# Eight instead of five feed-forward pairs per layer by halves, finer down pieces, and a reordered first projection

## The chip, the cores and the metric

The program runs on one core of one Trainium2 chip. The metric is device time in microseconds (us) for one execution. Shares are of TensorE (PE, with its weight loads PEld), VectorE (DVE), ScalarE (ACT), GpSimd (POOL) and SyncE (SP, which only issues loads).

## The reference, cut to what matters

```python
D_MODEL, SEQ, DEPTH, D_FF, FFN_CONV = 1024, 512, 2, 3072, 3
def _conv_ffn(x, norm, w_up, conv_w, conv_b, w_down):
    h = _rmsnorm(x, norm)
    u = jnp.einsum('btd,df->btf', h, w_up)                    # 1024 -> 2 x 3072
    gate = _causal_dwconv(u[..., :D_FF], conv_w, conv_b)      # three taps over the tokens
    hid = jax.nn.gelu(gate, approximate=True) * u[..., D_FF:]
    return jnp.einsum('btf,fd->btd', hid, w_down)             # 3072 -> 1024
def reference(x, ...):
    for layer in range(DEPTH):
        x = x + (_rglru_block if layer == 0 else _rwkv7_block)(x, ...)   # the mixer
        x = x + _conv_ffn(x, ffn_norm[layer], ...)
    return _rmsnorm(x, final_norm)
```

All is float32, for one batch of 512 tokens.

## The kernel before

A float32 product is made of three fast ones: a weight tile and an operand tile are each split into a high part (`wh`, `hi`, made on ACT by L121 or L742) and the rest (`wl`, `lo`, made on DVE by L125 or L743), and `mm3` (L81) multiplies high by high, high by low and low by high. Weights come in tiles of 512 KB into slots of 4 KB per partition (`b4`, `N4` = 21 slots), by loads on SP's queue in the order of a list, `plan`. A tile is loaded when a slot is free, and a slot is freed when the split's two halves, or the products of `wh` and `wl`, have been read.

The feed-forward stage of a layer goes through 12 **pairs** n of 256 gate and 256 value outputs. A `Whole` pair has four products, G0, U0, G1, U1 (each 24 matmuls of 512 columns). A `Halves` pair (n in `HALVES`) makes the same from seven products of 24 matmuls of 256 columns, numbered 1 to 7 (Strassen's scheme in a seven-product form over two halves of the tokens, of the inputs and of gate and value); for these the operands are made once per layer (`operands`), and the weight tiles of products 5, 6, 3 and 4 are sums of two pieces: for 5 and 4 the second piece is added by a DMA that accumulates (on POOL's queue, L207), for 3 by another one (L747), and for 6 DVE adds (L736). Before, pairs 3, 5, 7, 9 and 11 go by halves.

After every second pair, a **down** step multiplies 4 blocks of the hidden values (`hid`) of an earlier pair of pairs with `w_down`, for two groups g of 512 outputs each, in 96 matmuls; the last has 8 blocks. Behind the first 24 matmuls of it (`between`) stand products 3 and 4 of the pair. Its results are added to `x` (layer 0, L858) or `xtok` (layer 1, L847) on DVE. When product 4 has ended, DVE makes the gate (`gpad` L777, then the conv's `cv` L689), multiplies (`s` by `ge`, L782) and splits the hidden values (`hid`, L784).

`ahead(j)` writes the splits of the products up to the j-th into ACT's and DVE's queues. A scheduler sets the final order on each engine from this order and its own estimates; instructions that are pinned keep their order. Each engine runs its queue strictly in order.

At the start, blocks of `x` and pieces of `lru_w_in` land in turn; for each block ACT and DVE make a scaled, split operand `xs` (L324, L325) and add its squares to `sqacc` (L339, L340). The first group of four output blocks is then 96 matmuls, in four pieces c of two input blocks. Four tiny products with `inv_d` (`ssq`, L347) sum the squares, POOL takes the root, and `rbc` (L359) spreads it; with that DVE scales the results into `u` (L487).

Of the kernel before, what the change touches and what calls it, by code (L numbers as in the profile page):

```python
# [27 lines left out]
N4 = 21  # L28
WARM = 17

HALVES = (3, 5, 7, 9, 11)
# [40 lines left out]
class Kernel:  # L72
# [4 lines left out]
    def mm3(self, ps, w, x, start, stop, more=False):  # L77
# [4 lines left out]
        mm(wh, xh, start=start, stop=False)  # L82
        mm(wh, xl, start=False, stop=False)
        mm(wl, xh, start=False, stop=stop)
# [34 lines left out]
    def split(self, src, hi, lo, dve=False, pin=False):  # L119
# [5 lines left out]
        self.pin(self.nc.vector.tensor_tensor(lo, src, hi.bitcast(F32), ALU.subtract))  # L125
# [5 lines left out]
    def plan_weights(self):  # L131
        I = self.I
        plan = []
        self.quads = []
# [14 lines left out]
        def ffn(l):  # L149
            up, dn = ("ffn_w_up", (l,)), ("ffn_w_down", (l,))  # L150

            def gu(six):


                for n in range(2 * six, 2 * six + 2):
                    self.quads.append(len(plan))
                    a = lambda i, j: piece(up, j * 512, (1 - i) * DFF + n * 256, 4)
                    if n in HALVES:
                        for first, more in (((0, 0), None), ((1, 1), (1, 0)), ((0, 1), None), ((1, 0), (0, 0)), ((1, 1), None)):
                            plan.append((a(*first), 4, True, more and a(*more)))  # L160
                    else:
                        for i, j in ((1, 0), (0, 0), (1, 1), (0, 1)):
                            plan.append((a(i, j), 4, False, None))
                self.quads.append(len(plan))

            def dd(row, n):
                for g in range(2):
# [43 lines left out]
    def weights_split(self, upto, pin=False, between=None):  # L211
        while self.n_split < min(upto, len(self.plan)):
# [9 lines left out]
            for j in range(k) if i == 0 else [slice(0, k)]:  # L222
                self.split(raw[:, j], hi[:, j], lo[:, j], pin=pin)
                if j == 0:
                    between()
            self.splitted[i] = (hi, lo)
            self.n_split += 1
# [10 lines left out]
    def project_gen(self, xs, evac, nob=4, kb=8, kc=2, join=2, early=None, x0=0, ahead=2):  # L238
# [4 lines left out]
        for cs in [[c] for c in range(n - join)] + [list(range(max(n - join, 0), n))]:  # L243
            first = early and cs[0] == 0
            ws = [self.next_weights(1 if first else ahead) for _ in cs]
            if first:

                (wh, wl), = ws
                for o in range(nob):
                    self.mm3(pss[o], (wh[:, 0, o * P : (o + 1) * P], wl[:, 0, o * P : (o + 1) * P]), xs[0], True, False)  # L250
# [91 lines left out]
    def norm_end(self, rbs):  # L342
# [6 lines left out]
        nc.vector.tensor_scalar(ms, ps[:, :4], EPS, None, ALU.add)  # L349
# [16 lines left out]
    def load_x(self):  # L366
# [3 lines left out]
        nc.scalar.dma_start(self.x[:, 0], xT[:, 0])  # L370
        self.weights_load(1)
        nc.sync.dma_start(self.x[:, 1], xT[:, 1])
# [17 lines left out]
    def lru(self):  # L390
        nc, tc, I = self.nc, self.tc, self.I
        xs, block = self.load_x()
        with tc.tile_pool(name="lru", bufs=1) as pool:
# [5 lines left out]
            def blocks():  # L399
                for cb in range(2, KB):  # L400
                    block(cb)
                    self.squares(cb - 2)
                    yield 1
                for cb in range(KB - 2, KB):
                    self.squares(cb)
                    yield 1

# [14 lines left out]
            def gate_weights():  # L422

                lam = self.vec("lru_lambda", 0, 8)
# [3 lines left out]
                nc.vector.tensor_scalar(s, y, 2.0, None, ALU.add)  # L428
# [16 lines left out]
                bu = self.vec("lru_b_in", 8, 8)  # L445
# [5 lines left out]
                self.pin(nc.vector.tensor_scalar(nb, bu, -1.0, None, ALU.mult))  # L451
# [9 lines left out]
                self.split(graw, gh, gl)  # L461
                yield 1

            st, us, rbs = {}, {}, []

            def scale():
                root = self.norm_end(rbs)
                for step in (0, 1, 0, 0, 1):
                    if step:
                        next(root)  # L470
                    yield 1

            def first(c):
                if c == 1:
                    self.drain()
                    self.push(scale(), 1)
                    self.push(gate_weights())
                elif c == 2:
                    while not rbs:
                        self.background(1, 1)  # L480
                elif c == 3:
                    self.starting = False
# [74 lines left out]
            for g in range(2):  # L557
                self.project(xs, lambda o, ps: take(g * 4 + o, ps), after=None if g else first, rate=1.2, rate1=0 if g else 1.2, join=2 if g else 1,
                             early=None if g else lambda: block(1))
# [23 lines left out]
    def ffn(self, l, xs, finish, after=None):  # L583
        nc, tc = self.nc, self.tc
        last = l == 1
        with tc.tile_pool(name=f"ffn{l}", bufs=1) as pool:
# [72 lines left out]

            def hidden(n):  # L660
# [14 lines left out]
            class Pair:  # L675

                def __init__(pair, n):
                    pair.n, pair.gp = n, gpads[n % 2]
                    pair.w, pair.bank, pair.s = {}, {}, {}
# [45 lines left out]
            class Halves(Pair):  # L725

                order = ((1, 5, 6, 2, 7), (3, 4))

                def weights(pair, p):
                    i = quads[pair.n]  # L730
                    if p == 1:
                        self.weights_load(i + 4)
                        pair.f = dict(zip((1, 5, 2, 7), [self.loaded.pop(i + j) for j in range(4)]))
# [8 lines left out]
                    nc.scalar.copy(hi, f[p])  # L742
                    tt(lo, f[p], hi.bitcast(F32), ALU.subtract)  # L743
                    pair.w[p] = hi, lo
                    if p == 6:
# [3 lines left out]
                def product(pair, p):  # L749
# [5 lines left out]
                    for e in range(2):  # L755
                        c = slice(e * P, e * P + P)
                        for k in range(4):
                            self.mm3(ps[:, e], (hi[:, k, c], lo[:, k, c]), op[p][k], bool(name) and e + k == 0, e + k == 4, more=not name)
# [3 lines left out]
                    if p in (1, 6, 7):  # L762
                        s[p] = two(t("s", 7))
                        nc.scalar.copy(s[p], bank["A"])
                    if p == 2:
                        tt(s[1], s[1], bank["D"], ALU.add)
# [20 lines left out]
            starts = [self.quads[l * 18 + m] for m in range(18)]  # L787
# [1014 lines left out]
```

## Time and profile before

| | us |
|---|---|
| median of 3 runs (1277.37 to 1277.41) | 1277.37 |
| the profiled execution | 1278.56 |
| its span | 1276.9 |
| PE busy in the span | 1254.6 |
| DVE, ACT, POOL busy | 931.7, 639.0, 109.6 |

The profiled execution lies 1.2 us above the median, and 1.7 us above its own span. PE is at work in nearly all of the span, so a stage's length is, where PE has no gap, the sum of its matmuls. The feed-forward stage of layer 0 lies at about 195 to 540 us of the span, that of layer 1 at about 890 to 1240; between them is the RWKV mixer, ahead of them the LRU mixer.

### The profile page before, as it was taken

How to read it: one execution, taken by the hardware profiler on the slowest of the kernel's cores; microseconds unless marked ns; L12 is line 12 of the kernel's file. 1: busy time of each engine (PE TensorE's matmuls, PEld its weight loads, DVE VectorE, ACT ScalarE, POOL GpSimd, SP SyncE). 2: the span in 40 equal slices, each digit the busy share in tenths (PEclk: the TensorE clock that was granted, in tenths of full speed). 3: DMA queues.
4: the chain of work that ended last, by engine and by line, in shares of the span. 5: the costliest groups of instructions: out<-in, count | busy, mean ns of one | idle time of the engine just before them, and what ended most of it. 6: DMA issues, size and time to landing. Idle time of an engine off the chain costs nothing.

```text
span 1276.9 us, 22237 instructions
## 1 busy us (share of the span) xinstructions
PE 1254.6 (98%) x9213; PEld 1062.6 (83%) x9213; DVE 931.7 (73%) x1408; ACT 639.0 (50%) x978; POOL 109.6 (9%) x186
## 2 busy tenths in 40 slices
PE   8999999999999999999999899999999999999998
PEld 7777888989898989877778798778889888988886
DVE  6998678767676767789999967777876666666654
ACT  6697455434343434559845356545753434343442
POOL 0000000000000000010012145310000000000000
PEclk9999999999999999999999999999999999999999
DMA  6322334445454544413222112222435363535431
GB/s 223 99 83 83 99 119 113 156 108 166 99 175 89 182 83 137 149 50 109 67 75 68 35 63 88 69 72 83 134 82 185 79 188 77 190 76 190 97 126 66
DMA packets 43045, 141.42 MB, mean 111 GB/s; under 512 B 5600, under 2 KB 7904, under 8 KB 42816
## 3 DMA queue, kind: packets, MB, share of 16 engines
q1 hardware_dynamic: 37760, 122.44, 29.3%
q0 software_dynamic: 4464, 16.25, 7.4%
q8 instruction: 72, 1.18, 0.4%
q10 hardware_dynamic: 720, 1.31, 0.3%
q14 instruction: 29, 0.24, 0.1%
HBM read 135.46 MB, written 4.52 MB: 110 GB/s over the span
## 4 chain that ended last, share of the span: by engine, by line
PE 43%; DVE 6%; ACT 3%; issue 1%; POOL 0%; POOLq 0%; ACTq 0%; DVEq 0%
PE accU L81 6%; PE accG L81 6%; PE acc L81 5%; PE accA L81 4%; PE acc L842 3%; PE acc L844 3%; PE acc L843 3%; PE accF L81 2%; DVE X L1301 1%; PE accD L81 1%; PE s L1415 1%; DVE DA L1299 1%; PE acc L1247 1%; DVE wl L125 1%; PE pd L1497 1%
## 5 line engine op out<-in xcount | busy, mean ns | idle before, releaser
L125 DVE TENSOR_TENSOR wl<-raw,wh 128x1024 fp32r<-128x1024 f32 (+1 forms) x161 | 194.5, 1213 | 123.2 <-ACT wh L121 103.0
L121 ACT CAST wh<-raw 128x1024 fp32r<-128x1024 f32 (+1 forms) x161 | 166.2, 1044 | 180.0 <-PE acc L81 43.2
L81 PE MATMUL accG<-xs,wh 128*128 128x512 f32 x448 | 138.6, 391 | 0.0
L81 PE MATMUL accU<-xs,wh 128*128 128x512 f32 x448 | 138.5, 390 | 0.0
L81 PE MATMUL acc<-hid,wh 128*128 128x512 f32 x384 | 117.8, 389 | 0.0
L743 DVE TENSOR_TENSOR lo<-raw,hi 128x1024 fp32r<-128x1024 f32 x70 | 85.4, 1222 | 39.4 <-PE accU L81 32.0
L742 ACT CAST hi<-raw 128x1024 fp32r<-128x1024 f32 x70 | 73.7, 1054 | 60.5 <-PE accU L81 25.3
L81 PEld LDWEIGHTS accU<-xs,wh 128*128 128x128 f32 x448 | 83.7, 188 | 17.1
L81 PEld LDWEIGHTS accG<-xs,wh 128*128 128x128 f32 x448 | 83.6, 188 | 17.1
L81 PE MATMUL accU<-xs,wl 128*128 128x512 f32 x224 | 87.2, 389 | 0.0
L81 PE MATMUL accG<-xs,wl 128*128 128x512 f32 x224 | 87.2, 389 | 0.0
L81 PE MATMUL accA<-xt,hi 128*128 128x256 f32 x480 | 83.6, 277 | 0.0
L81 PE MATMUL acc<-xs,wh 128*128 128x512 f32 x256 | 82.5, 401 | 0.8 <-ACT xs L324 0.8
L81 PEld LDWEIGHTS acc<-hid,wh 128*128 128x128 f32 x384 | 71.3, 188 | 14.3
L689 DVE SCALAR_TENSOR_TENSOR cv<-gpad,pv,cv 128x512 f32<-128x512 f32 x96 | 69.1, 748 | 13.1 <-ACT cv L687 12.7
L842 PE MATMUL acc<-wh,hid 128*128 128x512 f32 (+1 forms) x200 | 76.8, 384 | 0.0
L844 PE MATMUL acc<-wl,hid 128*128 128x512 f32 (+1 forms) x200 | 76.8, 384 | 0.0
L843 PE MATMUL acc<-wh,hid 128*128 128x512 f32 (+1 forms) x200 | 76.8, 384 | 0.0
L81 PE MATMUL acc<-hid,wl 128*128 128x512 f32 x192 | 74.2, 389 | 0.0
L81 PEld LDWEIGHTS accA<-xt,hi 128*128 128x128 f32 x480 | 72.6, 188 | 0.0
L81 PE MATMUL accA<-xt,lo 128*128 128x256 f32 x240 | 66.4, 277 | 0.0
L81 PE MATMUL acc<-mix,wh 128*128 128x512 f32 x192 | 59.8, 393 | 1.6 <-ACT wh L121 1.6
(374 smaller groups left out, 2864.3 us busy)
## 6 DMA issues: line engine op xcount, KB each, us to landing
raw<-in_weights_dram SPq DMA_DIRECT2D x209, 512.0 KB, 3.6
raw<-in_weights_dram POOLq DMA_DIRECT2D x30, 512.0 KB, 5.3
xd<-x SPq DMA_DIRECT2D x8, 256.0 KB, 2.3
AR<-xd SPq DMA_DIRECT2D x1, 2048.0 KB, 8.6
x<-in_xT_dram SPq DMA_DIRECT2D x3, 512.0 KB, 8.0
out_dram<-xtok ACTq DMA_DIRECT2D x4, 256.0 KB, 2.1
out_dram<-xtok SPq DMA_DIRECT2D x4, 256.0 KB, 2.0
raw<-in_weights_dram SPq DMA_DIRECT2D x2, 256.0 KB, 4.2
```

The lines of the kernel that those rows point to most:

```text
L81: mm = lambda *a, **kw: self.nc.tensor.matmul(ps, *a, skip_group_check=more, **kw)
L121: put = (self.nc.vector.tensor_copy if dve else self.nc.scalar.copy)(hi, src)
L125: self.pin(self.nc.vector.tensor_tensor(lo, src, hi.bitcast(F32), ALU.subtract))
L689: nc.vector.scalar_tensor_tensor(cv, pair.gp[:, e, j : j + T], cw(j), cv, ALU.mult, ALU.add)
L742: nc.scalar.copy(hi, f[p])
L743: tt(lo, f[p], hi.bitcast(F32), ALU.subtract)
L842: nc.tensor.matmul(ps, hh[:, s], wh[:, k, m], start=kk == 0, stop=False)
L843: nc.tensor.matmul(ps, hl[:, s], wh[:, k, m], start=False, stop=False)
L844: nc.tensor.matmul(ps, hh[:, s], wl[:, k, m], start=False, stop=kk == blocks - 1)
L1247: nc.tensor.matmul(ps, hh[:, s], wh[:, k, :], start=kk + b % 2 == 0, stop=False)
L1299: nc.vector.tensor_tensor(w, A[:, s + 1 :, s : s + 1].to_broadcast([P, n, j]), X[:, s : s + 1, 0:j].to_broadcast([P, n, j]), ALU.mult)
L1301: nc.vector.tensor_tensor(X[:, s + 1 :, 0:j], X[:, s + 1 :, 0:j], w, ALU.add)
```

## The change

- `HALVES` gets 4, 6 and 8 besides: 8 of 12 pairs of each layer go by halves.
- The down step that stood after every second pair is cut in two: behind each pair from 3 to 9 (and behind pair 2) comes one group of 512 outputs, 48 matmuls: 24 between products 7 and 3, and 24 after product 4.
- Of a pair by halves, the order of products is 1, 2, 6, 5, 7 and 3, 4, where it was 1, 5, 6, 2, 7 and 3, 4. Edges of order without a semaphore (`behind`) fix some places on DVE and ACT: the sum for product 6 behind `lo2`, `lo7` behind the sum of products 1 and 2, `lo3` behind a weight split, the first down result behind the next pair's sum.
- The scratch for DMA descriptors is given as 4096 bytes, and `N4` is 24 slots.
- At the start, the first half of the first weight tile is rounded on DVE, block 1 of `x` comes by ACT's queue, the first block's products are ordered by kind, the squares of all blocks stand behind the operands of all blocks, and `ssq` moves from the middle of the third piece to behind the first output block of the fourth. Results that end before the root is there wait in a list (`taken`).

```diff
-N4 = 21
+N4 = 24
-HALVES = (3, 5, 7, 9, 11)
+HALVES = (3, 4, 5, 6, 7, 8, 9, 11)
...
-            gu(0)
-            for six in range(1, 6):
-                gu(six)
-                if six < 5:
-                    dd((six - 1) * 512, 4)
-            dd(2048, 8)
+            for n in range(12):
+                gu(n)
+                if 2 <= n < 10:
+                    dd((n // 2 - 1) * 512, 4, (n % 2,))
+            dd(2048, 8, (0, 1))
...
-        nc.scalar.dma_start(self.x[:, 0], xT[:, 0])
+        for cb in range(2):
+            nc.scalar.dma_start(self.x[:, cb], xT[:, cb])
...
                     block(cb)
-                    self.squares(cb - 2)
                     yield 1
-                for cb in range(KB - 2, KB):
+                for cb in range(KB):
                     self.squares(cb)
                     yield 1
...
+            def taken(o, ps):
+                held.append((o, ps))
+                if o == 0:
+                    self.need("squares")
+                    self.weights_split(6)
+                    next(root)
                     self.push(gate_weights())
+                elif o == 2:
+                    next(root)
+                while rbs and held:
+                    take(*held.pop(0))
...
-                order = ((1, 5, 6, 2, 7), (3, 4))
+                order = ((1, 2, 6, 5, 7), (3, 4))
...
                     if p == 6:
-                        tt(f[1], f[5], f[1], ALU.add)
+                        pair.sum = tt(f[1], f[5], f[1], ALU.add)
+                        behind(pair.sum, pair.at[2][1])
...
-            for n in range(3, 12, 2):
+            down(0, 0, 4, between)
+            ahead(at[0] + 2)
+            for n in (*range(3, 10), 11):
...
+                def between():
+                    products((n, 3))
+                    cap[0] = len(seq)
+                    if following:
+                        self.weights_load(quads[n + 1] + 4)
+                    products((n, 4))
+                    if following:
+                        ahead(at[0] + 3)
+                        held.append(pairs[n + 1].sum)
...
+                    down(n % 2, (n // 2 - 1) * 4, 4, between)
...
-    nc = _bacc.Bacc("TRN2", target_bir_lowering=False, num_devices=1)
+    nc = _bacc.Bacc("TRN2", target_bir_lowering=False, num_devices=1, dynamic_dma_scratch_size=4096)
```

Three places show what moves. The first is PE's queue in the first group of the first projection (`acc_136` to `acc_139` are its four output blocks; `xs_178`, `xs_187` are the operands of its third piece before, `xs_193`, `xs_202` those of its fourth after). Before:

```order
L81 MATMUL acc_137<-xs_187,wh_193 128x512 x2
L81 MATMUL acc_137<-xs_187,wl_194 128x512
L347 MATMUL ssq<-inv_d,sqacc 128x1 x4
L81 MATMUL acc_138<-xs_178,wh_193 128x512 x2
L81 MATMUL acc_138<-xs_178,wl_194 128x512
```

After:

```order
L81 MATMUL acc_136<-xs_202,wh_226 128x512 x2
L81 MATMUL acc_136<-xs_202,wl_227 128x512
L349 MATMUL ssq<-inv_d,sqacc 128x1 x4
L81 MATMUL acc_137<-xs_193,wh_226 128x512 x2
L81 MATMUL acc_137<-xs_193,wl_227 128x512
```

`ssq` stood behind 60 of the 96 matmuls, and now stands behind 78.

The second is DVE's queue around the first scaled results, `u`. Before:

```order
L486 COPY u<-nb 128x3 x4
L487 TENSOR_TENSOR u<-acc_136,rb 128x512
L125 TENSOR_TENSOR wl_326<-raw_239,wh_325 128x1024
L487 TENSOR_TENSOR u<-acc_137,rb 128x512
L493 TENSOR_SCALAR xr<-u,pv,cb_133 128x512
L487 TENSOR_TENSOR u<-acc_138,rb 128x512
L125 TENSOR_TENSOR wl_376<-raw_323,wh_375 128x1024
L487 TENSOR_TENSOR u<-acc_139,rb 128x512
```

After:

```order
L127 TENSOR_TENSOR wl_415<-raw_375,wh_414 128x1024
L441 TENSOR_TENSOR sp_131<-sp_131,sps 128x8
L442 TENSOR_SCALAR sp_131<-sp_131 128x8
L443 TENSOR_SCALAR sps<-pv 128x8
L444 TENSOR_TENSOR sp_131<-sp_131,sps 128x8
L127 TENSOR_TENSOR wl_467<-raw_412,wh_466 128x1024
L485 TENSOR_TENSOR u<-acc_136,rb 128x512
L485 TENSOR_TENSOR u<-acc_137,rb 128x512
L485 TENSOR_TENSOR u<-acc_138,rb 128x512
```

The four weight splits of the second group (the first two, `wl_272` and `wl_282`, stand further ahead, between the last addition of squares and `ms`, which takes the result of `ssq`) now all stand ahead of the first `u`, where they stood among and behind the `u`. Ten small instructions of 8 and 48 elements went behind the first `u`.

The third is DVE's queue behind product 4 of a pair by halves, in layer 0 (`wl` is a split for the down step, `lo` one for a product by halves, `x<-x,acc` adds a down result). Before, behind pair 3:

```order
L777 SCALAR_TENSOR_TENSOR gpad_1365<-accA,rb 128x2x256
L125 TENSOR_TENSOR wl_2278<-raw_2217,wh_2277 128x1024
L689 SCALAR_TENSOR_TENSOR cv<-gpad_1365,pv,cv 128x512 x4
L858 TENSOR_TENSOR x<-x,acc_2074 128x512
L858 TENSOR_TENSOR x<-x,acc_2075 128x512
L782 TENSOR_TENSOR s<-s,ge 128x512 x2
L858 TENSOR_TENSOR x<-x,acc_2076 128x512
L784 TENSOR_TENSOR hid<-s,hid 128x2x256 x2
L858 TENSOR_TENSOR x<-x,acc_2077 128x512
```

After, right behind the `gpad` of pair 5 (the three `lo` up to `lo_2883` are those of products 1, 2 and 6 of pair 6, `raw_2769` becomes the sum for 6, and `lo_2943` is that of product 5):

```order
L743 TENSOR_TENSOR lo_2831<-raw_2769,hi_2830 128x1024
L743 TENSOR_TENSOR lo_2835<-raw_2825,hi_2834 128x1024
L689 SCALAR_TENSOR_TENSOR cv<-gpad_1365,pv,cv 128x512 x4
L736 TENSOR_TENSOR raw_2769<-raw_2766,raw_2769 128x1024
L792 TENSOR_TENSOR s<-s,ge 128x512 x2
L743 TENSOR_TENSOR lo_2883<-raw_2769,hi_2882 128x1024
L794 TENSOR_TENSOR hid<-s,hid 128x2x256 x2
L871 TENSOR_TENSOR x<-x,acc_2771 128x512
L871 TENSOR_TENSOR x<-x,acc_2772 128x512
L871 TENSOR_TENSOR x<-x,acc_2773 128x512
L871 TENSOR_TENSOR x<-x,acc_2774 128x512
L743 TENSOR_TENSOR lo_2943<-raw_2766,hi_2942 128x1024
```

Between `gpad` and the `lo` of product 5 there are now two splits for products 1 and 2, the sum, a third split and all four additions to `x`. The same row stands behind pairs 5 to 8 of each layer, with `xtok` for `x` in layer 1; behind pairs 3 and 4 the first `lo` stands ahead of `gpad`.

## Rows read from the trace of the kernel before

**Rows 1.** The page, part 1: busy us, share of the span, instructions.

```profile
PE 1254.6 (98%) x9213; PEld 1062.6 (83%) x9213; DVE 931.7 (73%) x1408; ACT 639.0 (50%) x978; POOL 109.6 (9%) x186
```

**Rows 2.** Nine windows of 40 us in both feed-forward stages: busy us by engine, clock.

```profile
235.00:275.00 40.00, 40.00 (x209) 34.36 (x209) 24.60 (x32) 13.65 (x16) 1.73 (x2) 1.00 0.54 158
...
sum 360.00, PE 360.00 PEld 313.73 DVE 250.41 ACT 155.99 POOL 13.52; mean PE 40.00 PEld 34.86 DVE 27.82 ACT 17.33 POOL 1.50
```

**Rows 3.** Windows, PE alone: whole pair; products 1, 6, 2; 24 down matmuls; product 4.

```profile
264.05:285.81 21.76, 21.76 (x98) 1.00 0.44 95
222.72:225.59 2.87, 2.87 (x26) 1.00 0.03 7
...
228.33:231.05 2.72, 2.72 (x27) 1.00 0.61 170
231.05:233.91 2.86, 2.86 (x27) 1.00 0.62 199
...
236.65:242.10 5.45, 5.45 (x26) 1.00 0.73 256
...
244.97:247.71 2.74, 2.74 (x26) 1.00 0.46 102
```

**Rows 4.** Windows, PE alone: the seven products of pair 3, summed.

```profile
sum 19.54, PE 19.54; mean PE 2.79
```

**Rows 5.** Timeline of DVE behind product 4 of pair 3: start, us, what.

```profile
247.91 0.69 DVE L777 SCALAR_TENSOR_TENSOR gpad<-accA,rb 128x512 f32<-128x512 f32 x1 [0.31 <-PE accA L81]
248.52 1.22 DVE L125 TENSOR_TENSOR wl<-raw,wh 128x1024 fp32r<-128x1024 f32 x1
249.65 2.73 DVE L689 SCALAR_TENSOR_TENSOR cv<-gpad,pv,cv 128x512 f32<-128x512 f32 x4
252.30 1.28 DVE L858 TENSOR_TENSOR x<-x,acc 128x512 f32<-128x512 f32 x2
253.50 1.29 DVE L782 TENSOR_TENSOR s<-s,ge 128x512 f32<-128x512 f32 x2
254.70 0.69 DVE L858 TENSOR_TENSOR x<-x,acc 128x512 f32<-128x512 f32 x1
255.30 1.29 DVE L784 TENSOR_TENSOR hid<-s,hid 128x512 fp32r<-128x512 f32 x2
256.50 1.28 DVE L858 TENSOR_TENSOR x<-x,acc 128x512 f32<-128x512 f32 x2
```

**Rows 6.** Groups of DVE's instructions in layer 1's stage: busy us, mean ns.

```profile
L743 DVE TENSOR_TENSOR lo<-raw,hi 128x1024 fp32r<-128x1024 f32 x31 | 37.9, 1222 | 19.8 <-PE accU L81 16.0 <-ACT hi L742 2.9
L847 DVE SCALAR_TENSOR_TENSOR xtok<-acc,rs,xtok 128x512 f32<-128x512 f32 x32 | 23.2, 744 | 11.6 <-PE acc L844 11.6
```

**Rows 7.** DMA issues: engine, count, size, median us from issue to landing.

```profile
raw<-in_weights_dram SPq DMA_DIRECT2D x209, 512.0 KB, 3.6
raw<-in_weights_dram POOLq DMA_DIRECT2D x30, 512.0 KB, 5.3
```

**Rows 8.** Windows at the start: us, busy PE, PEld, DVE, ACT, POOL, clock, DMA.

```profile
20.60:22.68 2.08, 1.04 (x9) 0.89 (x9) 1.94 (x3) 1.85 (x6) 0.00 (x0) 1.00 0.05 22
22.68:26.18 3.50, 3.50 (x11) 2.76 (x10) 3.02 (x19) 0.00 (x0) 1.03 (x1) 0.52 0.49 157
27.94:33.38 5.44, 5.44 (x27) 4.52 (x26) 3.73 (x7) 4.49 (x5) 0.00 (x0) 1.00 0.14 39
...
40.00:80.00 40.00, 40.00 (x180) 29.15 (x180) 37.98 (x59) 34.98 (x49) 0.00 (x0) 1.00 0.30 93
```

**Rows 9.** Timeline of PE at the start: the sums of squares.

```profile
21.79 1.05 PE L347 MATMUL ssq<-inv_d,sqacc 128*128 128x1 f32 x8 [1.04 <-DVE sqacc L340]
```

**Rows 10.** Timeline of DVE at the start: before and at the first scaled result.

```profile
19.46 2.28 DVE L340 TENSOR_TENSOR sqacc<-sqacc,sq 128x512 f32<-128x512 f32 x3
...
26.26 0.17 DVE L442 TENSOR_SCALAR nsp<-sp 128x8 f32<-128x8 f32 x1
...
29.68 0.69 DVE L487 TENSOR_TENSOR u<-acc,rb 128x512 f32<-128x512 f32 x1 [1.71 <-PE acc L81]
```

More of the change, by code (lines that the diff above doesn't have):

```diff
@@ L222, in weights_split @@
             for j in range(k) if i == 0 else [slice(0, k)]:
-                self.split(raw[:, j], hi[:, j], lo[:, j], pin=pin)
+                put = self.split(raw[:, j], hi[:, j], lo[:, j], dve=i == 0 and j == 0, pin=pin)
                 if j == 0:
@@ L248, in project_gen @@
                 (wh, wl), = ws
-                for o in range(nob):
-                    self.mm3(pss[o], (wh[:, 0, o * P : (o + 1) * P], wl[:, 0, o * P : (o + 1) * P]), xs[0], True, False)
+                for part, (w, x) in enumerate(((wh, xs[0][0]), (wl, xs[0][0]), (wh, xs[0][1]))):
+                    for o in range(nob):
+                        ins = self.nc.tensor.matmul(pss[o], w[:, 0, o * P : (o + 1) * P], x, start=part == 0, stop=False)
+                        self.tc.keep_in_program_order(ins)
                 early()
@@ L461, in gate_weights @@
                 self.split(graw, gh, gl)
+                self.starting = False
                 yield 1
             st, us, rbs = {}, {}, []
[L466 to L476, printed above, removed]
-                    self.push(gate_weights())
[L478 to L482, printed above, removed]
+            root = self.norm_end(rbs)
+            held = []
+            def taken(o, ps):
[4 more added lines that the diff above has]
+                    next(root)
+                    self.push(gate_weights())
+                elif o == 2:
+                    next(root)
+                while rbs and held:
+                    take(*held.pop(0))
             def take(b, ps):
@@ L557, in lru @@
             for g in range(2):
-                self.project(xs, lambda o, ps: take(g * 4 + o, ps), after=None if g else first, rate=1.2, rate1=0 if g else 1.2, join=2 if g else 1,
-                             early=None if g else lambda: block(1))
+                self.project(xs, (lambda o, ps: take(4 + o, ps)) if g else taken, rate=1.2, join=2 if g else 1, early=None if g else lambda: block(1))
                 for b in (0, 1, 2, 3) if g == 0 else (4, 5):
@@ L658, in ffn, with behind @@
             op = {}
+            def behind(ins, prev):
+                tc.add_manual_dep(ins.ins, prev.ins.name, NOSYNC, reason="order")
             def hidden(n):
@@ L784, in product @@
                             tt(pair.hid[:, :, 1, h], x, pair.hid[:, :, 0, h].bitcast(F32), ALU.subtract)
-            starts = [self.quads[l * 18 + m] for m in range(18)]
-            quads = [starts[n // 2 * 3 + n % 2] for n in range(12)]
-            behind = [starts[n // 2 * 3 + 2] for n in range(12)]
+            quads = [self.quads[l, n] for n in range(12)]
             pairs, hids = {}, []
```

190 lines of the change are left out of this document (110 added, 80 removed).

## The prediction

> **What bounds the kernel now.** I read the page's engine shares first: PE is busy for 1254.6 us of the span, DVE for 931.7 [rows 1]. Since that is an average, the windows come next: nine of 40 us each, taken from both feed-forward stages, hold 360.00 us of PE work in 360.00 us at clock 1.00, and DVE is busy in 250.41 of them [rows 2]. So these stages, about 690 us together, are as long as their matmuls, and a matmul less is time less as long as nothing PE waits for comes late. The start is another matter: PE works 1.04 of 2.08 us and then 3.50 us at clock 0.52 [rows 8]; and from 40 to 80 us DVE is busy for 37.98 us of 40 [rows 8], so a gain of PE at the start counts there only as far as DVE's work also comes earlier.
>
> **Pairs 4, 6 and 8 by halves.** A whole pair takes PE 21.76 us [rows 3]; the seven products of a pair by halves take 19.54 [rows 4]. Each pair saves 2.22 us. Three pairs in each of two layers: 6 x 2.22 = **13.3 us**. The other order of products doesn't change their number. The down matmuls are the same ones in pieces of 24, 5.45 us each [rows 3]; the second group's pieces of 48 were already joined. Both kinds run without a gap today, so the cut is costed at nothing on PE, bounds 0 and 1 us.
>
> What hides the rest must now be checked, since the steps are closer. One step is 19.54 + 2 x 5.45 = 30.4 us of PE. DVE has in it seven `lo`, one sum and two `wl` (ten instructions of 1.22 us [rows 6], the sum taken as one of them), four `cv`, and some 14 to 16 of 512 columns at 0.60 to 0.74: about 12.2 + 2.7 + 10 = 25 us, or 82%. It fits as a sum; what matters is the order within the step.
>
> The tight place stands behind product 4 (third piece of the order). Measured from the end of product 4, which is the start of the second down piece (247.71 [rows 3]), by the pitches from one start to the next in [rows 5]: `gpad` begins at 0.20 and takes 0.61; `lo1` and `lo2` at 1.13 each (the pitch of `wl`, same shape), four `cv` 2.65, the sum 1.13, two `s` by `ge` 1.20, `lo6` 1.13, two `hid` 1.20, four additions to `x` at 0.60. `lo5` starts at 0.20 + 0.61 + 2.26 + 2.65 + 1.13 + 1.20 + 1.13 + 1.20 + 2.40 = 12.78 and ends at 14.0. PE reaches product 5 after the down piece, products 1, 2 and 6: 5.45 + 2.87 + 2.86 + 2.72 = 13.90 [rows 3], and reads `lo5` with its third matmul, 0.2 us later. So in layer 0 it is just in time, with 0 to 0.1 us lost. In layer 1 the additions are L847, 744 ns against about 690 [rows 6, 5]: 4 x 0.06 = 0.2 us later, so about 0.2 to 0.3 us is lost. That row stands behind four pairs of each layer (behind pairs 3 and 4 the first `lo` comes ahead of `gpad`, 1.13 us of slack): 4 x 0.05 + 4 x 0.25 = **1.2 us** taken. The bounds are 0 (an engine's idle in `gpad`'s place hides it) and, if every instruction were paid at its whole duration instead of at the pitch, the rival below.
>
> The next deadlines in the step by the same pitches: `lo7` ends at 12.78 + 1.13 + 0.60 + 1.22 = 15.7, and product 7 starts at 13.90 + 2.74 = 16.6: 0.9 us to spare. `lo3` ends some 1 us before the first down piece does. The loads on SP's queue: product 5's raw tile may load when product 5 of the pair before has been read, some 13.7 us before product 4 ends (2.74 + 5.45 + 2.87 + 2.74); it needs 3.6 us on SP and 5.3 on POOL [rows 7], so it is there 4.8 us before product 4 ends, and the sum asks for it 5.7 us after that: 10 us to spare. Each pair by halves has three accumulating loads on POOL's queue, 30 for ten pairs [rows 7] and 48 for sixteen; on that queue little else stands in these stages. These are costed at nothing. Other instructions queued behind a late tile would be the whole DVE row above; that is the rival on the slower side.
>
> **The 24 slots and the smaller scratch.** The slots let loads go earlier; with PE never waiting for a load in the stages [rows 2] that is worth nothing there, and in the mixers it only moves the order: 0, bounds -1.5 and +1.5. No row shows what a scratch of 4096 bytes does: bounds 0 and the slower rival's price; 0 taken, since 5.3 us per accumulating load [rows 7] leaves POOL's queue idle for about half of a step of 30.4.
>
> **The start.** PE waits 1.04 us for the last sum of squares and then runs 3.50 us at half clock [rows 8, 9], which loses 3.50 x 0.48 = 1.68. With `ssq` behind 78 matmuls instead of 60, it comes 18 x 0.227 = 4.1 us later on PE, while the squares end later too: DVE does one split (1.13) and half a tile's rounding more ahead of them, 19.46 + 2.28 + 1.5 = 23.2 [rows 10, 5], against `ssq` at about 20.7 + 4.1 = 24.8. So no wait, and no clock falls: PE gains 2.7 us. On DVE, four splits move ahead of the first `u` (4 x 1.13 = 4.5 us), ten small instructions behind it (26.26 to 29.68 - 1.71 = 27.97 holds fifteen small ones [rows 10]: about 1.1 us). The idle 1.71 us before the first `u` takes in part of it: the first `u` comes 4.5 - 1.1 - 1.7 = 1.7 us later than 29.68, and behind it stand 4.5 - 1.1 = 3.4 us less. DVE's work from there comes 1.7 us earlier. From 40 us on DVE is the fuller engine, so its figure counts: **-1.7**, bounds -4 (PE's gain, and the idle time in DVE's first 20 us used up) and 0 (the root's chain stands behind two splits; its end then sets the first `u`); below that, +1.7 if the clock falls in the new place as it did at 22.68.
>
> **The sum.** Against the profiled execution: 1278.6 - 13.3 + 1.2 - 1.7 = 1264.8; against the median, which is 1.2 us lower, 1277.4 - 13.8 = **1263.6**.
>
> **Rivals.**
> (A) DVE's row behind product 4 sets the pace. If the row costs whole durations (0.69, 1.22, 2.73, 1.29 and so on [rows 5, 6]), `lo5` ends at 0.2 + 0.69 + 4 x 1.22 + 2.73 + 2 x 1.29 + 4 x 0.69 + 1.22 = 15.1, and PE waits about 1.0 us in layer 0 and 1.2 in layer 1, in four steps each, 8.8 us. A third of it again for the steps with less slack gives 10 to 12, so about 1263.6 - 1.2 + 11 = 1273.4, from 1270 to 1276. For it: the margin is at zero, and a PE that waited lost its clock once [rows 8]. Against: in [rows 5] nine instructions of the same kinds start one behind the other at less than their durations, with no idle time between.
> [...]
> [...] By the row [rows 7], three loads of 5.3 us in a step of 30.4 don't pile up, but no row excludes a wait of POOL for scratch: (B) gets 8 in 100.
> (C) The start gives nothing, or the clock falls again: 1265.3 to 1267.
> (D) The stages lose nothing, and the start gives its full 4: 1277.4 - 13.3 - 4 = 1260.1; with the mixers' 1.5, 1258.6.
> (E) That the change doesn't do what it says: pairs stay whole. The order of PE's instructions speaks against it; 0.
>
> **How the numbers follow.** Forecast 0.55 (1261 to 1266), (C) 0.15, (D) 0.08, (A) 0.14, (B) 0.08. The range 1259.0 to 1273.0 takes in the forecast, (C), nearly all of (D) and about half of (A). About 0.2%, 2.6 us, can be told from no change: faster is below 1274.8, slower above 1279.9. Faster: forecast, (C), (D) and three fifths of (A), 0.86; same, the rest of (A), 0.06; slower, (B), 0.08.
>
> **What would show it.** Right: in the feed-forward windows PE still has 40.00 of 40; pairs 4, 6 and 8 take 19.5 us; at most 0.3 us of PE waiting for `lo` at product 5, four times a layer, more in layer 1; at the start no half clock in the 20s, and the first `u` near 31.4 us. Wrong: PE idle before product 5 of 1 us or more (A); DVE idle in front of the sum with a DMA as releaser (B); the clock at 0.5 again around 25 to 30 us (C). The prediction fails above all if the row behind product 4 has more in it than these pitches, since it has no slack.

## The result, and the profile after

The changed kernel takes 1281.86 us (median of nine runs), the one before 1277.39: a ratio of 1.0033, with a 95% interval of 1.0024 to 1.0042. It is slower by 0.33%, where 1263.6 was forecast. The profiled executions are 1282.94 and 1278.56 us, with spans of 1281.2 and 1276.9.

The page's first part, after (rows 1 answer to it):

```profile
PE 1248.3 (97%) x9645; PEld 1076.6 (84%) x9645; DVE 963.6 (75%) x1451; ACT 654.9 (51%) x1013; POOL 124.0 (10%) x204
```

PE is busy for 6.3 us less, not for 13.3, and its gaps are 10.6 us longer. To see where, I cut both spans at the same six places of PE's program: the first product of the feed-forward stage of layer 0 (155.56 us before, and not about 195 as said above); the end of product 4 of its last pair; the first product of the lora's second step (behind the last down step); the first product of the second feed-forward stage; the end of its last product 4; the end. The windows, with busy time by engine, clock and DMA, before:

```profile
0.00:155.56 155.56, 150.31 (x658) 117.16 (x659) 126.19 (x204) 107.09 (x151) 1.73 (x7) 0.99 0.34 114
155.56:500.09 344.53, 344.53 (x1938) 302.21 (x1936) 237.80 (x314) 146.12 (x187) 15.21 (x16) 1.00 0.47 132
500.09:551.37 51.28, 51.28 (x235) 42.23 (x233) 39.42 (x55) 25.39 (x37) 1.03 (x1) 1.00 0.33 114
551.37:881.42 330.05, 319.42 (x4229) 262.65 (x4228) 279.25 (x511) 194.42 (x380) 73.68 (x141) 1.00 0.23 72
881.42:1231.36 349.94, 349.94 (x1970) 305.65 (x1968) 226.33 (x288) 152.31 (x197) 15.65 (x17) 1.00 0.47 133
```

and after:

```profile
0.00:157.34 157.34, 151.15 (x658) 119.25 (x659) 126.20 (x205) 106.25 (x150) 1.73 (x7) 0.99 0.35 116
157.34:497.93 340.59, 339.17 (x2154) 307.14 (x2152) 249.76 (x331) 152.28 (x202) 23.12 (x25) 1.00 0.57 152
497.93:554.52 56.59, 53.74 (x234) 43.08 (x233) 42.16 (x58) 27.82 (x39) 1.03 (x1) 0.97 0.32 104
554.52:888.03 333.51, 320.37 (x4230) 263.50 (x4228) 282.75 (x513) 194.85 (x381) 72.21 (x141) 0.99 0.23 71
888.03:1235.33 347.30, 344.72 (x2186) 310.93 (x2185) 238.65 (x308) 159.20 (x214) 23.61 (x26) 1.00 0.57 150
```

| stretch | before | after | difference | forecast |
|---|---|---|---|---|
| first mixer | 155.56 | 157.34 | +1.8 | -1.7 |
| pairs of layer 0 | 344.53 | 340.59 | -3.9 | -6.7 + 0.2 |
| last down step of layer 0 | 51.28 | 56.59 | +5.3 | 0 |
| RWKV mixer | 330.05 | 333.51 | +3.5 | 0 (bounds 1.5) |
| pairs of layer 1 | 349.94 | 347.30 | -2.6 | -6.7 + 1.0 |
| the rest | 45.54 | 45.87 | +0.3 | 0 |

The pairs gain half of what they should; two stretches that the diff hardly touches lose more than that. These are single executions, the changed one 1.1 us above its median. In it the granted clock is 0.5 for 3.4 us at three places ahead of the end: in the first mixer, the last down step and the RWKV mixer; before, it is so once, at 22.8 us.

**The wait at product 5.** PE's timeline at product 5 of pair 7, after:

```profile
366.01 0.39 PE L81 MATMUL accF<-xt,hi 128*128 128x256 f32 x2
366.86 0.39 PE L81 MATMUL accF<-xt,lo 128*128 128x256 f32 x1 [0.47 <-DVE lo L743]
```

The third matmul starts 0.85 us after the first, where 0.23 would do. DVE's row ahead of it:

```profile
352.94 0.69 DVE L787 SCALAR_TENSOR_TENSOR gpad<-accA,rb 128x512 f32<-128x512 f32 x1 [1.33 <-PE accA L81]
353.55 2.35 DVE L743 TENSOR_TENSOR lo<-raw,hi 128x1024 fp32r<-128x1024 f32 x2
355.82 2.73 DVE L689 SCALAR_TENSOR_TENSOR cv<-gpad,pv,cv 128x512 f32<-128x512 f32 x4
358.47 1.21 DVE L736 TENSOR_TENSOR raw<-raw,raw 128x1024 f32<-128x1024 f32 x1
...
363.20 2.47 DVE L871 TENSOR_TENSOR x<-x,acc 128x512 f32<-128x512 f32 x4
365.59 1.22 DVE L743 TENSOR_TENSOR lo<-raw,hi 128x1024 fp32r<-128x1024 f32 x1
```

No idle time stands in front of the sum, so the accumulated tile is in time. Product 4 ended at 352.74; `lo5` starts 12.85 us after it, where the pitches of [rows 5] had given 12.78. The row was right. PE's side was not: product 5 starts 13.27 us after product 4's end and not 13.90, because part of the second down piece has run earlier, inside product 3 of pair 6:

```profile
346.44 0.40 PE L81 MATMUL accF<-xs,hi 128*128 128x256 f32 x2
346.68 0.63 PE L81 MATMUL acc<-hid,wh 128*128 128x512 f32 x2
347.14 0.39 PE L81 MATMUL acc<-hid,wl 128*128 128x512 f32 x1
347.37 0.28 PE L81 MATMUL accF<-xs,lo 128*128 128x256 f32 x1
```

Three matmuls of the down piece (0.69 us) stand between the second and third of product 3. They delay product 4, from which DVE's row starts, but not the time at which product 5 is due. Four steps of each layer wait: product 5 takes 3.03 and three times 3.48 us in layer 0, 3.59 to 3.80 in layer 1, where 2.72 would do; together it is 2.6 and 3.9 us longer.

**The last down step.** There PE waits 1.94 us for ACT and then goes on at a lower clock. The windows of the wait and of what follows, and ACT's timeline:

```profile
508.94:511.26 2.32, 0.38 (x2) 0.00 (x0) 1.33 (x4) 1.56 (x2) 0.00 (x0) 1.00 0.01 4
511.26:515.50 4.24, 4.24 (x12) 3.33 (x13) 2.65 (x3) 1.04 (x1) 0.00 (x0) 0.61 0.00 0
```

```profile
507.11 1.22 ACT L793 CAST hid<-s 128x512 fp32r<-128x512 f32 x2 [1.43 <-DVE s L792]
509.65 0.62 ACT L123 CAST g<-lt 128x512 fp32r<-128x512 f32 x1 [1.31 <-DVE lt L939]
510.17 1.04 ACT L123 CAST wh<-raw 128x1024 fp32r<-128x1024 f32 x1
```

`wh` of the last piece stands behind the hidden values and behind a lora weight (`g`), which waits for DVE. Before, that `wh` stood ahead of the hidden values and PE had no gap:

```profile
506.05 1.05 ACT L121 CAST wh<-raw 128x1024 fp32r<-128x1024 f32 x1
507.00 1.14 ACT L783 CAST hid<-s 128x512 fp32r<-128x512 f32 x2
```

The wait costs 1.9 us, and twelve matmuls in 4.24 us instead of 2.7 at clock 0.61 another 1.5.

**The start.** PE's first matmuls, after:

```profile
6.57 2.08 PE L251 MATMUL acc<-xs,wh 128*128 128x512 f32 x4 [1.24 <-ACT xs L326]
8.44 1.91 PE L251 MATMUL acc<-xs,wl 128*128 128x512 f32 x4
```

They begin 0.47 us later than before, and nine of them take 3.9 us, most 427 ns each. The wait for the squares is gone, as forecast, but `ssq` comes at 26.18 instead of the 24.8 worked out, and DVE's first `u` at 33.18, not 31.4:

```profile
33.18 1.88 DVE L485 TENSOR_TENSOR u<-acc,rb 128x512 f32<-128x512 f32 x3
```

At the end of the first mixer stand the products with `out`. There PE waits twice, and the clock falls (the last row is a window):

```profile
110.54 0.50 PE L81 MATMUL acc<-out,wh 128*128 128x512 f32 x1 [0.90 <-ACT out L123]
112.28 0.50 PE L81 MATMUL acc<-out,wh 128*128 128x512 f32 x1 [1.24 <-DVE out L127]
112.28:116.28 4.00, 4.00 (x11) 3.14 (x12) 4.00 (x7) 2.98 (x5) 0.00 (x0) 0.57 0.11 42
```

From the first product with `out` to the first pair PE takes 46.8 us, where it took 46.0 before.

### The profile page after: what moved, and what is told of

Its sections match the earlier page's. It is cut to its first block, busy times and chain, and to the rows that moved or that the text cites. A ratio compares the mean times of both kernels' runs of the same rounds, so it can differ in the third digit from the quotient of the medians.

```text
span 1281.2 us, 23259 instructions
## 1 busy us (share of the span) xinstructions
PE 1248.3 (97%) x9645; PEld 1076.6 (84%) x9645; DVE 963.6 (75%) x1451; ACT 654.9 (51%) x1013; POOL 124.0 (10%) x204
## 4 chain that ended last, share of the span: by engine, by line
PE 35%; DVE 12%; ACT 3%; issue 2%; POOL 1%; POOLq 0%; DVEq 0%; ACTq 0%
PE accA L81 5%; PE acc L81 4%; PE accF L81 4%; PE accU L81 3%; PE accG L81 3%; PE acc L857 3%; PE acc L859 3%; PE acc L858 3%; DVE X L1346 1%; DVE lo L743 1%; DVE wl L127 1%; PE accD L81 1%; DVE DA L1344 1%; DVE cv L689 1%; PE s L1460 1%
## 5 line engine op out<-in xcount | busy, mean ns | idle before, releaser
L127 DVE TENSOR_TENSOR wl<-raw,wh 128x1024 fp32r<-128x1024 f32 (+1 forms) x137 | 164.8, 1213 | 26.0 <-ACT wh L123 24.8
L743 DVE TENSOR_TENSOR lo<-raw,hi 128x1024 fp32r<-128x1024 f32 x112 | 134.7, 1219 | 15.5 <-ACT hi L743 15.4
L743 ACT CAST hi<-raw 128x1024 fp32r<-128x1024 f32 x112 | 113.5, 1050 | 40.4 <-DVE raw L736 19.3
L81 PE MATMUL accA<-xt,hi 128*128 128x256 f32 x768 | 133.9, 277 | 0.0
L81 PEld LDWEIGHTS accA<-xt,hi 128*128 128x128 f32 x768 | 116.2, 188 | 0.0
L81 PE MATMUL accA<-xt,lo 128*128 128x256 f32 x384 | 106.3, 277 | 0.0
L687 ACT ACTIVATE cv<-gpad,pv 128x512 f32<-128x512 f32 x48 | 37.5, 812 | 110.3 <-DVE gpad L787 97.5
L81 PE MATMUL accU<-xs,wh 128*128 128x512 f32 x256 | 79.5, 392 | 0.0
L81 PE MATMUL accG<-xs,wh 128*128 128x512 f32 x256 | 79.5, 392 | 0.0
L81 PEld LDWEIGHTS accA<-xt,lo 128*128 128x128 f32 x384 | 72.2, 188 | 0.0
```

The lines of the kernel that those rows point to most:

```text
L127: rest = self.nc.vector.tensor_tensor(lo, src, hi.bitcast(F32), ALU.subtract)
L687: nc.scalar.activation(cv, pair.gp[:, e, 0:T], AF.Identity, bias=self.vec(f"ffn_conv_b{l}", fb), scale=cw(0))
L743: pair.at[p] = nc.scalar.copy(hi, f[p]), tt(lo, f[p], hi.bitcast(F32), ALU.subtract)
```

## The experiments

My theory after the result: three orders lose the time, each at its own place: down matmuls inside product 3, the lora preparation inside the last pair's chain, and the new start. The rivals: the closer steps press on something shared (loads, POOL, slots), or DVE's row is longer than its pitches.

**1. The start of before, with the rest changed.** The hunks of the start are undone.

```diff
-                self.split(raw[:, j], hi[:, j], lo[:, j], dve=i == 0 and j == 0, pin=pin)
+                self.split(raw[:, j], hi[:, j], lo[:, j], pin=pin)
...
-                for cb in range(KB):
+                    self.squares(cb - 2)
+                for cb in range(KB - 2, KB):
```

> The changed kernel with its new start undone: first block, order of squares, place of the sums of squares and small instructions as before; pairs, down pieces, slots and scratch as changed. Theory (the start costs 1.8 us: half clock in its first nine matmuls, and DVE's first scaled result at 33.2 instead of 29.7 us): the first product of the feed-forward stage of layer 0 begins near 155.6 us, as before, and the time is 1280.1. Rival (the 1.8 us come from the mixer's own order under 24 slots, not from the start): it still begins at 157 and the time stays at 1281.9.

Measured 1277.78 us, a ratio of 1.0008 (0.9999 to 1.0017). The first pair begins at 154.46 us, 2.9 us earlier than with the new start and 1.1 earlier than before the change. So beside the 24 slots the new start costs time, and the old one even gains a little. More than forecast came back; part of it is in the last down step (55.13 us instead of 56.59), which this edit doesn't touch and which was 55.03 in experiment 2 as well. The wait there is the same in both (1.95 and 1.93 us), but the clock stayed at 1.00 behind it, so these 1.5 us are the clock's.

The clock at the products with `out` does go with the start. It is 0.5 for 3.4 us at 110 to 113 us in all eight traces of the changed program with the new start (after, experiments 2 to 6, 9 and 11), and 1.00 there in the three with the old one (1, 8 and 10), where the stretch takes 46.0 us again.

**2. The second half of each down piece held behind product 4.**

```diff
-                                 xs[x0 + kk], kk == 0, kk == kb - 1)
+                                 xs[x0 + kk], kk == 0, kk == kb - 1, pin=hold and (c, k) == (1, 0))
```

> The changed kernel, with the second half of each down piece held behind product 4 on PE; in the changed kernel one to five of its matmuls run inside product 3, so that product 4 ends up to 0.7 us later while product 5 is due at the same time. Theory (PE waits for the low part of product 5, which ends a fixed 14.0 us after product 4 in layer 0 and 14.3 in layer 1; 0.68 us of the wait come from these matmuls): the wait of 0.75 us falls to 0.1 and that of 0.85 to 1.0 us to 0.2 to 0.3 in each step, and the time by 4 to 5 us, to about 1277.4. Rival (the row on DVE costs more than its pitches): the waits keep their size, 1281.9.

Measured 1275.32 us, 0.9985 (0.9977 to 0.9994): one pinned order makes the changed kernel faster than the one before. The stages of the pairs:

```profile
156.13:494.67 338.54, 338.54 (x2154) 307.16 (x2152) 250.04 (x331) 151.93 (x202) 23.09 (x25) 1.00 0.58 153
883.18:1227.83 344.65, 344.46 (x2185) 310.88 (x2184) 238.83 (x308) 159.31 (x214) 23.58 (x26) 1.00 0.56 151
```

In layer 0 PE has no gap again, 2.0 us less than after the change; in layer 1, 2.65 less, with 0.19 us of idle. DVE's row is the same work; `lo5` starts at 363.60, 12.92 us after product 4's end. So it was the due time. The median is 6.5 us lower. Of the 7.6 us between the two profiled executions 4.7 are in these stages; the first mixer (1.2) and the last down step (1.6) were shorter in this one too.

**3. The additions to `x` behind `lo5`.**

```diff
-                        ahead(at[0] + 3)
-                        held.append(pairs[n + 1].sum)
+                        ahead(at[0] + 4)
+                        held.append(pairs[n + 1].at[5][1])
```

> The changed kernel, with the four additions of down results to the residual behind the low part of product 5 on DVE instead of ahead of it. Theory (these additions, 2.4 to 2.7 us, make product 5 late): no wait at product 5 is left, 6.4 us less, 1275.5, unless the low part of product 7, now the next in the row, comes late by up to 0.2 us a step (then 1276.5). Rival (the accumulated tile comes late, so that the sum on DVE waits): the wait stays, 1281.9.

Measured 1278.23 us, 0.9998 (0.9989 to 1.0007): 3.6 us back and not 6.4. The stages of the pairs give back 2.7 us. The wait at product 5 is gone, but the list of PE's waits in layer 0 has a new line (with 1.0 us more of the same in layer 1):

```profile
PE accA L81 <- ACT s L770: 0.7, 2, 0.4
```

With product 5 split earlier, the high part `hi5` goes into ACT's queue ahead of the copy that empties product 1's bank, and product 6, which wants that bank, starts late. Neither theory had this: the wait moved to the other engine.

**4. The weight splits of the last down step earlier.**

```diff
                 def between():
+                    if n == 11 and not last:
+                        self.weights_split(quads[n] + 9)
                     products((n, 3))
```

> The changed kernel, with all four weight splits of the first group of layer 0's last down step written ahead of products 3 and 4, so that none stands on ACT behind the split of the hidden values. Theory (PE waits 2.3 us for the fourth split, whose high part stands on ACT behind the hidden values and a lora weight, and then runs nine matmuls at half clock, 1.8 us): both go, 4.1 us less, 1277.8. Rival (the split is late because its tile is loaded late, for want of a slot): the wait stays, 1281.9.

Measured 1280.26 us, 1.0019 (1.001 to 1.0028): 1.6 us back and not 4.1. In the last down step no clock fell this time. `wh` is no longer late, but the next thing is:

```profile
PE acc L81 <- ACT hid L793: 1.6, 1, 1.6
```

The last quarter of the down step multiplies the hidden values of the last pair, and these too come late. So the place of the splits was a part of it only: the hidden values themselves come late.

**5. The lora preparation behind product 4.**

```diff
                     self.norm_begin()
-                    self.push(self.lora_weights())
                 down(0, 16, 8, between)
...
                     products((n, 4))
+                    if n == 11 and not last:
+                        self.push(self.lora_weights())
```

> The changed kernel, with the preparation of the lora weights in layer 0's last down step written behind product 4 of the last pair instead of ahead of product 3. Theory (this preparation stands on DVE and ACT inside the chain from product 4 to the hidden values, and both those and the fourth weight split come late because of it): the stretch from the end of product 4 to the first product of the lora's second step, 51.3 us before, 56.6 after the change and 54.5 with the splits alone moved, falls to 52 and the time to about 1277.5. Rival (the chain is too long even without it, 10.9 us from product 4 to the last quarter): it stays above 54, 1280.

Measured 1274.55 us, 0.9976 (0.9966 to 0.9987): 7.3 us back, more than expected. The last down step and the RWKV mixer:

```profile
497.05:549.36 52.31, 51.67 (x235) 41.94 (x233) 43.06 (x60) 27.40 (x39) 1.03 (x1) 1.00 0.32 107
549.36:879.37 330.01, 318.71 (x4229) 262.14 (x4228) 280.47 (x511) 193.92 (x380) 74.33 (x141) 1.00 0.23 72
```

The step takes 52.3 us at clock 1.00, 1.0 more than before the change, and the mixer behind it 330.0, as before. So the order of these few splits also cost the 3.5 us in the mixer. That both come back with this one edit is shown. Where the mixer loses most of them can be read too (in both fences the second row is a window). In the changed kernel:

```profile
647.12 1.20 PE L81 MATMUL acc<-mix,wh 128*128 128x512 f32 x4 [2.19 <-ACT wh L123]
648.70:652.11 3.41, 3.34 (x8) 2.66 (x9) 2.52 (x10) 2.53 (x5) 0.00 (x0) 0.50 0.00 0
```

Before:

```profile
640.81 1.20 PE L81 MATMUL acc<-mix,wh 128*128 128x512 f32 x4 [1.55 <-ACT wh L121]
640.81:645.00 4.19, 4.19 (x17) 3.18 (x18) 4.02 (x11) 1.84 (x2) 0.00 (x0) 1.00 0.00 0
```

This wait is 2.2 us with half clock behind it in all seven traces whose mixer takes 333 to 336 us (after, 1 to 4, 6 and 8), and 1.6 us without it in the six with 330. Two smaller waits ahead of it are longer in the seven as well (for `l2h` 0.7 to 1.2 us against none, for a `wl` 0.9 against 0.4). Which instruction on ACT makes them longer was not taken apart.

**6. 21 slots and the scratch of before.**

```diff
-N4 = 24
+N4 = 21
...
-num_devices=1, dynamic_dma_scratch_size=4096)
+num_devices=1)
```

> The changed kernel with 21 slots and the DMA scratch of before. Theory (slots and scratch matter little; the three late places are matters of order): the waits at product 5 stay at 0.75 and 0.85 to 1.0 us, the feed-forward stages stay within 1 us. Rival (the 24 slots let loads and preparations go earlier and so spoil the RWKV mixer's order, which is 3.5 us longer from the lora's second step to the second feed-forward stage): that stretch falls from 333.5 to 330 us, and the time to 1278.5. Rival on the other side (the halves need the slots): PE waits for weights in the feed-forward stages, and the time grows by 3 us or more.

Measured 1281.57 us, 1.0029 (1.0016 to 1.0041), as with 24. The waits at product 5 stay (4.3 us in all), the stages of the pairs are 341.08 and 346.91 us; the accumulating loads land 5.6 us after issue in both. Slots and scratch carry neither the gain nor the loss of the stages of the pairs and of the last down step. The two mixers, though, moved: the first pair begins at 154.88 us, 2.5 us earlier, and the RWKV mixer takes 335.6 us, 2.1 more, where the first rival wanted 330.

**7. The new start alone, in the kernel before.** Only the hunks of the start are applied.

```diff
-                self.split(raw[:, j], hi[:, j], lo[:, j], pin=pin)
+                put = self.split(raw[:, j], hi[:, j], lo[:, j], dve=i == 0 and j == 0, pin=pin)
...
-                for cb in range(KB - 2, KB):
+                for cb in range(KB):
```

> The kernel before with the new start alone. Theory (the start costs time by itself, since PE's first matmuls come 0.5 us later and run at half clock, and DVE's first scaled result later): the first product of the feed-forward stage of layer 0 begins at 156 to 157.5 us instead of 155.6, 1278.5 to 1279.3. Rival (the start gains what was forecast, and the loss came from elsewhere in the first mixer): 1275.7.

Measured 1277.71 us, 1.0002 (0.9994 to 1.0011): no difference. In the profiled execution the first pair begins at 154.25 us, 1.3 us earlier than before, and the mixer behind it is 0.4 longer. So alone the start does not lose, as my theory said, nor does it show the gain that was forecast. The first matmuls are as slow here as after the change, so they alone can't be what costs the time after it. The two waits at the products with `out` stand here too (0.90 and 1.24 us), but the clock stayed at 1.00:

```profile
110.67:114.67 4.00, 4.00 (x18) 3.32 (x19) 4.00 (x7) 2.97 (x5) 0.00 (x0) 1.00 0.01 4
```

The stretch from there to the first pair takes 45.3 us.

**8. Start of before, down pieces held, splits earlier and lora later.** The edits of experiments 1, 2, 4 and 5.

```diff
+                                 xs[x0 + kk], kk == 0, kk == kb - 1, pin=hold and (c, k) == (1, 0))
...
+                        self.weights_split(quads[n] + 9)
                     products((n, 3))
...
+                        self.push(self.lora_weights())
```

> The changed kernel with three edits together: the start of before, the second half of each down piece held behind product 4 on PE, and in layer 0's last down step the weight splits ahead of and the lora preparation behind products 3 and 4. If the three places are independent: 1281.9 less 4 (start), 6.5 (down pieces) and 4 to 5 (last down step), 1267. If one only hands its time to the next wait: 1271 or more.

Measured 1271.5 us, 0.9952 (0.994 to 0.9965). First mixer 154.03, pairs 338.90 and 344.67, last down step 52.77, but the RWKV mixer is 333.92 again: beside edit 5, edit 4 gives back what edit 5 won there (experiment 10 is the same without edit 4, at 330.11). The next three leave it out.

**9. Down pieces held, lora later.** The edits of experiments 2 and 5.

```diff
+                                 xs[x0 + kk], kk == 0, kk == kb - 1, pin=hold and (c, k) == (1, 0))
...
+                    if n == 11 and not last:
+                        self.push(self.lora_weights())
```

> The changed kernel, new start and 24 slots kept, with two orders changed: the second half of each down piece behind product 4, and the lora preparation behind product 4 of layer 0's last pair. If the two losses are independent: 1281.9 less 6.5 less 7.3, 1268; feed-forward stages 338.5 and 344.7 us, last down step 52.3, mixer 330.0. If one hands its time on: 1271 or more.

Measured 1269.24 us, 0.9937 (0.9924 to 0.9949). Pairs 338.56 and 344.69, last down step 52.34, mixer 330.10: the two losses add up, within 1.2 us.

**10. As 9, with the start of before.** The edits of experiments 1, 2 and 5.

> As the run before, with the start of the kernel before as well. Theory (with 24 slots the new start costs 1.5 to 3 us against the old one): the first feed-forward stage begins at 154.0 to 154.5 us instead of 156 to 157.4, and the time is 1265 to 1266.5. Rival (the start's cost is chance of the clock in single executions and evens out): within 1 us of the run before.

Measured 1267.44 us, 0.9925 (0.9911 to 0.9938), the fastest of all: 9.8 us below the kernel before of the same runs, 14.4 below the changed one. The same five stretches:

```profile
0.00:154.30 154.30, 149.33 (x657) 117.48 (x658) 126.07 (x204) 106.78 (x151) 1.75 (x7) 1.00 0.36 118
154.30:492.88 338.58, 338.58 (x2153) 307.18 (x2152) 250.06 (x330) 152.93 (x203) 23.13 (x25) 1.00 0.58 154
492.88:545.22 52.34, 51.70 (x234) 41.96 (x233) 43.07 (x60) 27.39 (x39) 1.03 (x1) 1.00 0.33 107
545.22:875.33 330.11, 319.05 (x4230) 262.40 (x4228) 280.60 (x511) 194.08 (x380) 74.52 (x141) 1.00 0.23 72
875.33:1220.01 344.68, 344.47 (x2185) 310.85 (x2184) 238.91 (x308) 159.52 (x214) 23.62 (x26) 1.00 0.56 151
```

**11. As 9, with 21 slots.** The edits of experiments 2, 5 and 6.

> As the first run of this group, new start kept, with 21 slots and the scratch of before. Theory (slots tell only at the start, where 24 of them let weights crowd the first 20 us: DMA share 0.91 with 24 slots and the new start, 0.72 to 0.75 with 21): the first feed-forward stage begins at 154.3 to 154.9 us, the rest as with 24 slots, 1266. Rival (the closer halves need the 24 slots): waits for weights in the feed-forward stages, 1270 or more.

Measured 1268.59 us, 0.9931 (0.9919 to 0.9943), and the first pair begins at 154.61 us instead of 156.08. The rest is as with 24 slots: the halves don't need them. The DMA share of the first 20 us, 0.72 with the new start and 21 slots and 0.91 with 24, goes with the later start; but the old start has 0.90 with 24 slots and loses nothing, so the share alone isn't the cause, and it stays open. The half clock at the products with `out` isn't it either, since it stands in this trace too; PE reaches these products at 107.81 us here and at 109.28 in experiment 9.

## Why the prediction was wrong, point by point

- **13.3 us from the pairs.** Right, to 0.3 us. With the order pinned the two stages are 6.0 and 5.3 us shorter (experiment 10), 11.2 together. What is missing stands at product 5, the next term; its windows in experiment 10, one of each layer:

```profile
362.80:365.67 2.87, 2.87 (x27) 1.00 0.28 54
1088.51:1091.61 3.10, 3.00 (x26) 1.00 0.13 25
```

In four steps of each layer product 5 still takes 2.87 or 2.88 us and 2.94 to 3.11, where 2.72 would do: 0.6 and 1.2 us.
- **1.2 us at product 5.** This step failed first. DVE's side was right to 0.1 us. PE's due time was put together from whole pieces, 5.45 + 2.87 + 2.86 + 2.72, in the order in which the code writes them. But nothing held the down matmuls behind product 4, and the order of PE's instructions after the change, which was there to be read before the result, has one to three of them inside product 3. The prediction read DVE's order there and not PE's. Product 5 was 2.6 and 3.9 us longer, 6.5 together; with the order pinned it is 1.8, so for the order that the prediction assumed its 1.2 was near. Rival (A) had 8.8 us at this place for another reason, and the reason was wrong: instructions were not paid at whole durations, by which `lo5` would have started 13.8 us after product 4's end, and it started at 12.85.
- **"Both kinds run without a gap today, so the cut is costed at nothing."** This step failed most, with 5.3 us in the last down step and 3.5 in the mixer behind, of which 1.5 and about 1.7 are half clock behind a wait. The prediction has no term for the last down step. It took the code there as unchanged, since the diff leaves its calls nearly alone, and did not read the order there. The splits of products 3 and 4 were now written ahead of the lora preparation, and this slid into the chain from product 4 to the hidden values (experiments 4 and 5). The bound of 1.5 us for the mixers, said to come from slots, had no row behind it; with 21 slots the RWKV mixer is no shorter (experiment 6).
- **-1.7 us at the start.** Wrong by 3.5 us in the profiled execution. The sum of DVE's work was fair (its last addition of squares ended at 23.6 us against 23.2 worked out). So were the times of `ssq` and of the first `u`, 24.8 and 31.4: in the five traces with this start whose first matmuls aren't slow they are 24.2 to 24.5 and 31.8 to 32.1. Slow first matmuls come and go between traces of the same start, and about 1 us goes with them: with 24 slots and this start, the first pair begins at 156.1 us in the three traces without them and at 156.9 to 157.4 in the three with. What failed is "So no wait, and no clock falls", which was worked out for the 20s alone. There it holds; the fall came at 112.8 us, behind the waits for `out`, and the stretch from there is 46.8 us long instead of 46.0 (45.3 where the clock stayed, experiment 7). Rival (C) had a fall, but at 25 to 30 us. With 24 slots the new start costs 1.8 us against the old one (9 and 10), alone in the old kernel nothing (7). Why PE reaches the products with `out` later with 24 slots (109.3 us, against 107.8 and 108.1 with 21, all without slow first matmuls) stays open.
- **Slots and scratch at nothing.** For the scratch, right: with 4096 bytes the accumulating loads land 5.6 to 6.6 us after issue, with the scratch of before 5.6 and 6.2 (experiments 6 and 11), and none of the 16 sums has a wait of DVE in front of it (after). All 48 accumulating loads of the changed kernel ran with 4096 bytes. For the slots, right in the stages of the pairs; the mixers moved by up to 2.5 us with them and the scratch (experiment 6). Rival (B), the slower side, a sum that waits for its load, did not happen: no run shows a load late for want of scratch, so its 0.08 was the author's estimate alone. The kernel came out slower for a cause that was no rival at all.
- **The range.** It was built from the feed-forward steps and the start. It had no term for a stretch in which only the scheduler's order changes, and this alone, 8.8 us, would have taken the forecast to its upper end.
- **A slip without effect.** 2.74 + 5.45 + 2.87 + 2.74 is 13.8 and not 13.7.

## What to carry to other kernels

When a change shortens the work of an engine that has no gaps, every due time must be read from that engine's own order after the change, not from the order of the code: here the first matmul of each of four output blocks, pinned in each down piece, was worth 4.7 us in the two stages. Code that the diff leaves alone may still be scheduled anew, so compare the order on all engines wherever a chain ends at a stage's boundary. And move one thing at a time there: of two edits that each shortened the last down step, one, put beside the other, undid its gain in the mixer behind. A trace is one execution: compare it with others before a lost clock or slow first matmuls are put down to an edit.

## What the runs showed of the hardware

A wait of PE cost more than its length in some of these traces, and the same wait did not in others. After 1.94 us of waiting in the last down step the granted clock of the next 4.24 us was 0.61, and matmuls of 227 ns took 427: another 1.5 us, nearly the wait again. It was so in experiments 3 and 6 as well, behind the same 1.9 us. In experiment 1, behind 1.95 us at the same place, the clock stayed at 1.00, and 19 matmuls ran in the time of twelve; in experiment 2 it stayed too:

```profile
508.70:512.94 4.24, 4.24 (x19) 3.50 (x20) 3.75 (x5) 1.53 (x2) 0.00 (x0) 1.00 0.02 8
```

In the RWKV mixer 2.2 us of waiting were followed by half clock in seven traces of seven, 1.6 us in none of six. At the products with `out`, 0.9 and 1.2 us a little apart were followed by it in eight of nine. The waits at product 5, 0.7 us at most, left the clock of the stages at 1.00:

```profile
PE accF L81 <- DVE lo L743: 4.0, 7, 0.7
```

At the start, ten matmuls took 4.00 us behind a wait of 1.24 us although the rows there read a clock of 1.00:

```profile
6.57:10.57 4.00, 4.00 (x10) 3.19 (x11) 3.25 (x5) 3.22 (x5) 0.00 (x0) 1.00 1.02 404
```

Of the thirteen traces six have five to eight matmuls of about 427 ns there, four of nine with the new start (after, 3, 4 and 7) and two of four with the old (1 and 10), so the new start alone isn't the reason. What held them is open.
